# A hybrid attention and RG-LRU block: other portions for the RG-LRU's background steps, another call for placing attention's first tiles

## The chip, the core and the metric

The kernel runs on one core of one Trainium2 chip. The metric is the device time of one execution in microseconds. TensorE (PE) multiplies, VectorE (DVE), ScalarE (ACT) and GpSimd (POOL) do the elementwise work, and all DMAs are issued on one queue, that of SyncE (SP), in order.

## What is computed

One transformer block over 2048 tokens of width 1024 with a context of 256 tokens, all in float32. One input projection gives queries, keys and values of a differential attention (4 heads, two maps per head of 64 dimensions, values of 128) and, for the other half of the width, the input u and the gate g of an RG-LRU. Cut to its core:

```python
q, k, v, u, g = split_proj(h @ w_in)              # and the same of the context
q, k = apply_rope(q, cos, sin), apply_rope(k, cos, sin)
s = einsum(q, k_all) * ATT_SCALE                  # two maps m per head
p = softmax(s); a = p[0] - lam * p[1]
o = diff_head_norm(a @ v_all)
# RG-LRU, both directions d, 512 channels
u = centred_conv(u, conv_w, conv_b)
r, i = sigmoid(u @ w_gates[d] + b_gates[d])       # in blocks of 64 channels
log_a = -8 * r * softplus(-lru_lambda[d])
h_t = exp(log_a) * h_(t-1) + sqrt(-expm1(2 * log_a)) * i * u
y_lru = (h_forward + h_backward) * gelu(g)
y = concat(o, y_lru) @ w_out
x = layer_norm(alpha * x + g1 * y)                # then a SwiGLU, and a second norm
```

## The kernel before

**Stages.** Norms, modulation and the projection to u take the first 210 us; the other projections run to 700 us with the RG-LRU behind them; attention runs from 700 to about 1420 us; the output projection and the two FFN products fill the rest. Every float32 product is made of three matmuls on values split into a high and a low part (`mm3`, L141 to L144), so all activations and weights are split: `hi` and `lo` by ACT (L209) and POOL (L210) behind a projection, weights by ACT (L173) and DVE (L174).

**Projections.** The tokens are four blocks of 512, X = blocks 2 and 3 first, then Y = blocks 0 and 1, each with its activations `ht` in SBUF (two tiles, loaded in four DMAs each). One projection of 128 columns over one block is 24 matmuls into a PSUM tile `ps_p` (values: `ps_v`, four per block and pair of heads). A q or k projection is evacuated by ACT (a copy `kf`) and DVE (rope: the shuffle L203, products L204 and L205, sum L206), then split and stored; a value only needs ACT and one DVE step (L249). X runs g, v, k, q (32 calls of a background function, `between_x`), then Y runs g (8 calls), then head by head k, v and q in 24 calls of `between`.

**Background.** The RG-LRU is a generator, `chain()`, over four blocks of 128 channels: convolution, gate weights, gates (matmuls `ps_g`, ACT L571, POOL L573), the recurrence (DVE L603 to L624, with four long scans L620, L623, L621, L624), and the output (L629, L643 to L646). Each step yields a cost; `pump(n)` takes steps until costs of n have been taken, so n is the portion that a call deals out. The costs are 67.4 for a channel block, 269.6 for four; then the generator says "drained" and holds until the g projections of Y are done, and its tail (`lru_out_y`, the lines L665 and L669, 10.8 for all four blocks) takes their output to `oy_d`.

**Handover.** `over_lru` takes what is left of the chain, closes the LRU's memory, lays attention's first tiles (`k0`, `k1`, `q0`, four `e`, the ring `aR`, PSUM `psS`) into the same place, and issues the loads of the first query; in later calls `early` takes 24 steps of the first scores, two each. A step is four matmuls `ps_s` (L846), a DVE pass (L848), and at the third step an exponent on ACT (L853); six steps make a tile of 128 queries, which POOL then turns into the difference of the two maps (L861, three L864). The product with the values (`pt`, then `po`, L920 to L927) of the first tile begins after 32 steps.

**What sets the order.** The program is written in the order of the code, but a scheduler with a model of the engines' times then places the instructions of each engine, so a step written earlier may run later, and DMAs are placed on SP's one queue in the same way.

Of the kernel before, what the change touches and what calls it, by code (L numbers as in the profile page):

```python
# [60 lines left out]
def kernel(ctx: ExitStack, tc: tile.TileContext, x, cx, prm_d, wa1, wa2, b_ada, w_in, w_v, lqk,  # L61
# [91 lines left out]
    with ExitStack() as s12:  # L153
# [26 lines left out]
        def load_tabs(b):  # L180
            ct = rp.tile([P, 512], F32, tag="ct", name="ct")
            st = rp.tile([P, 512], F32, tag="st_", name="st_")
            dma(ct, cos_d[:, b * 512:(b + 1) * 512])
            dma(st, sin_d[:, b * 512:(b + 1) * 512])
            tabs[b] = ct, st
# [523 lines left out]
        def pump(n):  # L709

            state["due"] += n
            paces.append((last["act"], last["dve"]))
            act, dve = paces[max(0, len(paces) - 1 - 1)]
            while state["due"] > 0:
                if state["end"] or (state["hold"] and not state["g_done"]):
                    state["due"] = 0
                    return
                try:
                    with tc.issue_after(act), tc.issue_after(dve):
                        cost = next(bg)  # L720
                    if cost == "drained":
                        state["hold"] = True
                    else:
                        state["due"] -= cost or 1.0
                except StopIteration:
                    state["end"] = True
# [39 lines left out]

        def between_x():
            next(fold, None)
            pump(5.5)

        X, Y = [2, 3], [0, 1]

# [6 lines left out]
        for b in Y:  # L779
            load_ht(b)  # L780
            load_tabs(b)
        run_units([("g", c, Y) for c in range(4)], lambda: pump(5.5))
        state["g_done"] = True

        slots = {}
# [93 lines left out]
        calls = [0]  # L879

        def between():
            calls[0] += 1
            if calls[0] < 14:
                pump(5)
            elif calls[0] == 14:
                over_lru()
            else:
                for _ in range(2):
                    early()
# [3 lines left out]
        def early():  # L893
            if left[0]:
                left[0] -= 1
                next(first)
# [400 lines left out]
    with ExitStack() as s6:  # L1297
# [40 lines left out]
        for n in range(32):  # L1338
            hf, i = n // 16, n % 16
            c = slice(hf * 512, (hf + 1) * 512)  # L1340
# [99 lines left out]
```

## Time and profile before

| | |
|---|---|
| median of three runs | 2962.98 us (2962.23 to 2969.71) |
| the profiled execution | 2965.58 us, span 2963.8 us |
| PE busy | 2776.1 us, 94% |
| DVE busy | 1955.0 us, 66% |
| ACT busy | 1407.1 us, 47% |
| POOL busy | 1421.9 us, 48% |

The page says where the time goes by engine; the chain of work that ended last lies on PE for 67% of the span. As averages over stages these shares don't say which engine is waited for between 200 and 740 us, where the change lies; this is read from the windows, waits and timelines in the section of rows below. All times are microseconds from the span's start.

### The profile page before, as it was taken

The numbers are of one execution on the slowest core, as the hardware profiler recorded it, in microseconds if no ns is written. First come the engines' busy times: TensorE is split into PE (matmuls) and PEld (weight loads), VectorE is DVE, ScalarE is ACT, GpSimd is POOL, SyncE is SP. The second block draws the span as 40 slices with busy tenths as digits, with TensorE's granted clock in tenths as the row PEclk, the third lists the DMA queues.
The fourth block names the chain that finished last, engine by engine and source line by source line (L and its number), as shares of the span: only waits on it lengthen the run. The fifth ranks groups of instructions, "written<-read, shape, count | busy, mean of one in ns | idle before, by whom it ended". The sixth has DMA issues, their size and how long they took to land.

```text
span 2963.8 us, 37341 instructions
## 1 busy us (share of the span) xinstructions
PE 2776.1 (94%) x13452; PEld 2316.7 (78%) x13452; DVE 1955.0 (66%) x3202; ACT 1407.1 (47%) x1907; POOL 1421.9 (48%) x891
## 2 busy tenths in 40 slices
PE   8989889878999999999985999999999998999998
PEld 4868767766899999887864888887888886887886
DVE  7755796487899989986886655558655545225554
ACT  3537568744777777763344333334333324113332
POOL 2014643455788888861535444445444433222443
PEclk9999999989999999999997999999999999999999
DMA  8874636366132312135563222223222218434542
GB/s 332 313 217 167 215 116 256 113 219 184 36 85 64 81 58 70 54 140 195 193 200 114 93 86 82 84 84 104 93 82 82 84 52 291 146 129 162 172 165 93
DMA packets 223193, 407.94 MB, mean 138 GB/s; under 512 B 20888, under 2 KB 110104, under 8 KB 220448
## 3 DMA queue, kind: packets, MB, share of 16 engines
q1 hardware_dynamic: 223008, 405.55, 41.2%
q8 instruction: 106, 1.74, 0.2%
q14 instruction: 79, 0.65, 0.1%
HBM read 281.74 MB, written 123.75 MB: 137 GB/s over the span
## 4 chain that ended last, share of the span: by engine, by line
PE 67%; DVE 7%; ACT 3%; DMA 3%; issue 1%; POOL 1%; SPq 0%; ACTq 0%; DVEq 0%; POOLq 0%
PE ps L143 9%; PE ps L144 9%; PE ps L142 9%; PE ps_s L846 8%; PE ps_f L142 5%; PE ps_f L143 5%; PE ps_f L144 5%; PE pt L927 4%; PE po L921 2%; PE po L922 2%; PE po L920 2%; DMA w2r<-in_w 1%; DVE e L848 1%; PE ps_w L1050 1%; PE ps_l L1050 1%
## 5 line engine op out<-in xcount | busy, mean ns | idle before, releaser
L848 DVE TENSOR_SCALAR_CACHE_REDUCE e<-ps_s 128x768 f32<-128x768 f32 x384 | 359.6, 951 | 37.7 <-PE ps_s L846 29.6
L864 POOL TENSOR_TENSOR a<-e,e 128x768 f32<-128x768 f32 x192 | 349.2, 1848 | 17.2 <-PE pt L927 12.5
L846 PE MATMUL ps_s<-k,q 128*128 128x384 f32 x1536 | 336.7, 351 | 15.1 <-DVE e L848 13.7
L853 ACT ACTIVATE e<-e,nm 128x2304 f32<-128x2304 f32 x128 | 285.3, 2229 | 51.8 <-DVE nm L852 48.7
L846 PEld LDWEIGHTS ps_s<-k,q 128*128 128x128 f32 x1536 | 267.9, 191 | 31.0 <-DVE e L848 23.9
L1324 POOL TENSOR_TENSOR hid<-hf,hid 128x1408 fp32r<-128x1408 f32 x32 | 104.8, 3276 | 293.9 <-ACT hid L1323 293.9
L931 ACT CAST ah<-pt 128x512 fp32r<-128x512 f32 x288 | 165.8, 582 | 127.7 <-PE pt L927 125.4
L932 DVE TENSOR_TENSOR al<-pt,ah 128x512 fp32r<-128x512 f32 x288 | 195.7, 685 | 33.7 <-ACT ah L931 33.4
L1323 ACT CAST hid<-hf 128x1408 fp32r<-128x1408 f32 x64 | 87.8, 1375 | 248.0 <-PE ps_f L144 232.0
L861 POOL TENSOR_SCALAR e<-e,rr,rn 128x2304 f32<-128x2304 f32 x64 | 146.4, 2287 | 92.5 <-DVE nm L852 49.6
L142 PE MATMUL ps_p<-ht,w 128*128 128x512 f32 (+1 forms) x416 | 162.8, 392 | 16.0 <-DVE kf L204 10.8
L927 PEld LDWEIGHTS pt<-ident,a 128*128 128x128 f32 x1152 | 144.5, 141 | 42.0 <-POOL a L864 3.3
L927 PE MATMUL pt<-ident,a 128*128 128x128 f32 x1152 | 174.7, 274 | 2.6 <-POOL a L864 2.4
L1189 POOL TENSOR_TENSOR s<-w1r 128x512 f32<-128x512 f32 x44 | 58.0, 1317 | 233.5 <-DMA w1r<-in_w 228.2
L144 PE MATMUL ps_p<-ht,w 128*128 128x512 f32 (+1 forms) x416 | 161.8, 390 | 8.2 <-DVE w L174 8.2
L143 PE MATMUL ps_p<-ht,w 128*128 128x512 f32 (+1 forms) x416 | 161.5, 388 | 0.0
L210 POOL TENSOR_TENSOR lo<-kf,hi 128x512 fp32r<-128x512 f32 (+1 forms) x36 | 58.7, 1632 | 176.5 <-ACT hi L209 140.8
L1194 POOL TENSOR_TENSOR s<-w1r,s 128x512 f32<-128x512 f32 x44 | 73.1, 1661 | 126.9 <-DVE w__15147 L1199 5.6
L920 PE MATMUL po<-ah,v 128*128 128x512 f32 x288 | 126.3, 438 | 0.6 <-ACT ah L931 0.6
L921 PE MATMUL po<-al,v 128*128 128x512 f32 x288 | 116.9, 406 | 3.1 <-DVE al L932 1.4
L922 PE MATMUL po<-ah,v 128*128 128x512 f32 x288 | 114.5, 398 | 0.0
L1324 DVE TENSOR_TENSOR hid<-hf,hid 128x1408 fp32r<-128x1408 f32 x32 | 54.4, 1701 | 86.2 <-ACT hid L1323 86.2
(3085 smaller groups left out, 8258.8 us busy)
## 6 DMA issues: line engine op xcount, KB each, us to landing
w1r<-in_w SPq DMA_DIRECT2D x88, 512.0 KB, 3.5
hf<-hid_d SPq DMA_DIRECT2D x64, 704.0 KB, 4.2
hid_d<-hid SPq DMA_DIRECT2D x88, 256.0 KB, 2.2
wraw<-in_w_in SPq DMA_DIRECT2D x32, 512.0 KB, 5.1
adaw<-in_wa SPq DMA_DIRECT2D x32, 512.0 KB, 4.7
q<-q_d SPq DMA_DIRECT2D x64, 256.0 KB, 4.9
oy<-oy_d SPq DMA_DIRECT2D x16, 1024.0 KB, 6.2
x<-in_x SPq DMA_DIRECT2D x24, 512.0 KB, 8.9
```

The costliest lines, as they stand in the source:

```text
L142: PE.matmul(ps, lhsT=lh, rhs=rh, start=start, stop=False)
L143: PE.matmul(ps, lhsT=lh, rhs=rl, start=False, stop=False)
L144: last["pe"] = PE.matmul(ps, lhsT=ll, rhs=rh, start=False, stop=stop).ins
L846: PE.matmul(ps[:, j, :384], lhsT=q[:, m, part, qt * P:(qt + 1) * P], rhs=kst[h, m][:, c0:c0 + 384], start=(part == 0), stop=(part == 1))
L848: V.tensor_scalar(et[:, cc * 768:(cc + 1) * 768].rearrange("p (a b) -> p a b", a=2), ps[:, :, :384], -0.125, None, ALU.mult, ALU.min, accu ...
L853: S.activation(et, et, AF.Exp, bias=nm[:, m:m + 1], scale=-1.0, accum_out=ss[m])
L864: last["a"] = G.tensor_tensor(a, es[0][:, g * 768:(g + 1) * 768], es[1][:, g * 768:(g + 1) * 768], ALU.add).ins
L920: PE.matmul(po, lhsT=vh, rhs=ah, start=(j == 0), stop=False)
L921: PE.matmul(po, lhsT=vh, rhs=al, start=False, stop=False)
L922: PE.matmul(po, lhsT=vl, rhs=ah, start=False, stop=(j == NKT - 1))
L927: PE.transpose(pt[:, qt * P:(qt + 1) * P], ath[h, b, qt, j // 6][:, (j % 6) * P:(j % 6 + 1) * P], ident)
L932: V.tensor_tensor(al, pt, ah.bitcast(F32), ALU.subtract)
```

## The change

Three numbers and one condition change. A call in X and in Y's g projections deals out portions of 7 and not 5.5 (32 + 8 calls: 280 of cost and not 220, where the whole chain has 280.4), a call in the rest of Y 6 and not 5, and `over_lru` stands at the eleventh of those calls and not at the fourteenth, so that `early` begins with the twelfth.

```diff
--- before.py
+++ after.py
@@ -766,7 +766,7 @@
 
         def between_x():
             next(fold, None)
-            pump(5.5)
+            pump(7)
 
         X, Y = [2, 3], [0, 1]
 
@@ -779,7 +779,7 @@
         for b in Y:
             load_ht(b)
             load_tabs(b)
-        run_units([("g", c, Y) for c in range(4)], lambda: pump(5.5))
+        run_units([("g", c, Y) for c in range(4)], lambda: pump(7))
         state["g_done"] = True
 
         slots = {}
@@ -880,9 +880,9 @@
 
         def between():
             calls[0] += 1
-            if calls[0] < 14:
-                pump(5)
-            elif calls[0] == 14:
+            if calls[0] < 11:
+                pump(6)
+            elif calls[0] == 11:
                 over_lru()
             else:
                 for _ in range(2):
```

The two programs hold the same work; the scheduler places it otherwise. Up to some 380 us the order is nearly the same. The gates of channel block 2 stood between the first and third projection of Y and now stand between the fourth and eighth; those of block 3 move from the fourteenth to sixteenth to the seventeenth to twentieth (of 32). Three places follow, each before and after.

DVE at the end of X's keys, where the scans of channel block 1 (`L621` forward half, `L624` backward half) meet the rope of the keys (L203 to L206) and a weight split (`L174`), before:

```order
L621 SCALAR_TENSOR_TENSOR gate_3081<-A_3310,gate_3081 128x2048
L206 TENSOR_TENSOR kf<-kf,sh 128x512
L624 SCALAR_TENSOR_TENSOR gate_3083<-A_3311,gate_3083 128x2048
L174 TENSOR_TENSOR w<-wraw,w 128x1024
L204 TENSOR_TENSOR kf<-ps_p,ct 128x512
L205 TENSOR_TENSOR sh<-sh,st__1992 128x512
L203 STREAM_SHUFFLE sh<-kf 128x512
L206 TENSOR_TENSOR kf<-kf,sh 128x512
```

and after, from the same scan on:

```order
L621 SCALAR_TENSOR_TENSOR gate_2830<-A_3096,gate_2830 128x2048
L204 TENSOR_TENSOR kf<-ps_p,ct 128x512
L205 TENSOR_TENSOR sh<-sh,st__1992 128x512
L174 TENSOR_TENSOR w<-wraw,w 128x1024
L624 SCALAR_TENSOR_TENSOR gate_2832<-A_3097,gate_2832 128x2048
L203 STREAM_SHUFFLE sh<-kf 128x512
L206 TENSOR_TENSOR kf<-kf,sh 128x512
L204 TENSOR_TENSOR kf<-ps_p,ct 128x512
```

One `L204`, with its `L205`, moved from behind `L624` and `L174` to directly behind `L621`; the next `L204` stands behind all of them.

A little later, where X ends, SP's queue changes too: the loads `ht` of Y's first block stood one by one among stores of queries and of RG-LRU output, and now three of four stand in a row directly behind the store `hs_d` of block 1's recurrence; those of the second block stay together, and the gate weights' loads `gr` go from ahead of them to behind. On PE the first projection of Y was cut by 48 gate matmuls in three pieces; it now stands whole (24), then 6 matmuls of the second block, then 19 of the first block's next projection.

DVE at the end of the RG-LRU: `L665` and `L643` are its last products, L203 to L206 rope of q and k, `L249` the evacuation of a value, `L174` a weight split. Before:

```order
L665 TENSOR_TENSOR gg<-hs,gg 128x1024
L204 TENSOR_TENSOR kf<-ps_p,ct 128x512
L205 TENSOR_TENSOR sh<-sh,st__4121 128x512
L203 STREAM_SHUFFLE sh<-kf 128x512
L665 TENSOR_TENSOR gg<-gate_4402,gg 128x1024
L206 TENSOR_TENSOR kf<-kf,sh 128x512
L643 TENSOR_TENSOR gg<-gate_4402,gg 128x512
L204 TENSOR_TENSOR kf<-ps_p,ct 128x512
L205 TENSOR_TENSOR sh<-sh,st__4112 128x512
L174 TENSOR_TENSOR w<-wraw,w 128x1024
L643 TENSOR_TENSOR gg<-gate_4402,gg 128x512
L665 TENSOR_TENSOR gg<-hs,gg 128x1024
```

and after, from the longer scans on:

```order
L621 SCALAR_TENSOR_TENSOR gate_4129<-A_4385,gate_4129 128x2048
L206 TENSOR_TENSOR kf<-kf,sh 128x512
L624 SCALAR_TENSOR_TENSOR gate_4131<-A_4386,gate_4131 128x2048
L249 TENSOR_TENSOR vl<-ps_v,vh 128x512
L174 TENSOR_TENSOR w<-wraw,w 128x1024
L665 TENSOR_TENSOR gg<-hs,gg 128x1024
L665 TENSOR_TENSOR gg<-gate_4129,gg 128x1024
L643 TENSOR_TENSOR gg<-gate_4129,gg 128x512 x2
L174 TENSOR_TENSOR w<-wraw,w 128x1024
L249 TENSOR_TENSOR vl<-ps_v,vh 128x512 x2
L665 TENSOR_TENSOR gg<-hs,gg 128x1024
```

Before, the last products stood among the rope steps of q and k projections; now they stand among value evacuations, directly behind the two scans.

The handover, PE's end of the projections (`ps_p`) and its first scores (`ps_s`), to the first product with the values (`po`), before:

```order
L144 MATMUL ps_p<-ht,w 128x512
L846 MATMUL ps_s<-k,q 128x384 x16
L927 MATMUL pt<-ident,a 128x128 x2
L846 MATMUL ps_s<-k,q 128x384 x32
L927 MATMUL pt<-ident,a 128x128 x2
L846 MATMUL ps_s<-k,q 128x384 x12
L927 MATMUL pt<-ident,a 128x128 x2
L846 MATMUL ps_s<-k,q 128x384 x36
L927 MATMUL pt<-ident,a 128x128 x2
L920 MATMUL po<-ah,v 128x512
```

and after:

```order
L144 MATMUL ps_p<-ht,w 128x512
L846 MATMUL ps_s<-k,q 128x384 x56
L927 MATMUL pt<-ident,a 128x128 x2
L846 MATMUL ps_s<-k,q 128x384 x12
L927 MATMUL pt<-ident,a 128x128 x2
L846 MATMUL ps_s<-k,q 128x384 x36
L927 MATMUL pt<-ident,a 128x128 x2
L846 MATMUL ps_s<-k,q 128x384 x12
L927 MATMUL pt<-ident,a 128x128 x2
L846 MATMUL ps_s<-k,q 128x384 x8
L920 MATMUL po<-ah,v 128x512
```

Before this point the order had four groups of eight `ps_s` among the last four projections; there are none now, and all scores stand behind the projections. SP's queue at the same place, with the loads of the first query (`q_d_72`) and keys (`k_d_68`), before:

```order
L70 DMA k_d_70<-lo 128x512 x2
L70 DMA v_d_77<-vh 256x1x256
L70 DMA wraw<-in_w_in 128x1024
L70 DMA v_d_77<-vh 256x1x256
L70 DMA q<-q_d_72 64x2x512 x4
L70 DMA v_d_77<-vl 256x1x256
L70 DMA k<-k_d_68 64x2304 x4
L70 DMA v_d_77<-vl 256x1x256
L70 DMA v_d_77<-vh 256x1x256 x2
L70 DMA v_d_77<-vl 256x1x256
```

and after:

```order
L70 DMA q_d_74<-hi 128x512
L70 DMA oy_d_78<-gg 128x512
L70 DMA oy_d_79<-gg 128x512
L70 DMA v_d_77<-vl 256x1x256
L70 DMA q_d_74<-lo 128x512
L70 DMA q_d_74<-hi 128x512
L70 DMA k_d_71<-hi 128x512
L70 DMA q<-q_d_72 64x2x512 x4
L70 DMA k<-k_d_68 64x2304 x4
```

The loads stood ahead of most value stores of the second pair of heads and of every store of `k_d_71`; now they stand behind the value stores and the first store of `k_d_71`, the keys of the last head, of the fourth-last projection.

## Rows read from the trace of the kernel before

**Rows 1.** Windows; time, busy us (instructions) of PE, PEld, DVE, ACT, POOL, clock, DMA share.

```profile
600.00:700.00 100.00, 84.47 (x433) 73.18 (x432) 78.37 (x91) 40.16 (x52) 42.20 (x22) 0.91 0.64 209
...
700.00:740.00 40.00, 27.27 (x109) 19.48 (x107) 28.48 (x66) 21.04 (x21) 32.70 (x21) 0.91 0.65 189
...
800.00:900.00 100.00, 100.00 (x606) 91.46 (x605) 90.56 (x208) 75.22 (x96) 83.66 (x53) 1.00 0.34 90
```

**Rows 2.** Waits of PE from 300 to 700 us (total, times, longest); durations of line L174.

```profile
PE ps_p L142 <- DVE kf L204: 10.8, 2, 8.6
...
PE ps_v L142 <- ACT w L173: 10.0, 2, 6.0
...
PE ps_p L144 <- DVE w L174: 7.4, 6, 2.4
...
PE ps_g L142 <- ACT gate L571: 4.3, 2, 3.3
...
L174 DVE TENSOR_TENSOR w<-wraw,w x28: 1204/1226/2741, 251.4 to 675.6; 128x1024 fp32r<-128x1024 f32 x28
```

**Rows 3.** Timelines of DVE, POOL, PE near 430 us; start, duration, instruction, idle time before.

```profile
417.78 4.81 DVE L621 TENSOR_TENSOR_SCAN gate<-A,gate 128x2048 f32<-128x2048 f32 x1
...
423.10 4.47 DVE L624 TENSOR_TENSOR_SCAN gate<-A,gate 128x2048 f32<-128x2048 f32 x1
...
427.49 2.22 DVE L174 TENSOR_TENSOR w<-wraw,w 128x1024 fp32r<-128x1024 f32 x1
...
429.63 0.68 DVE L204 TENSOR_TENSOR kf<-ps_p,ct 128x512 f32<-128x512 f32 x1
...
428.59 7.33 POOL L629 TENSOR_TENSOR gate<-gate,gate 128x512 f32<-128x512 f32 x4
...
430.45 0.77 PE L142 MATMUL ps_p<-ht,w 128*128 128x512 f32 x1 [8.60 <-DVE kf L204]
```

**Rows 4.** Timeline of PE at 457 us; the tile `ht`, 425 to 480 us.

```profile
457.82 0.50 PE L142 MATMUL ps_p<-ht,w 128*128 128x512 f32 x1 [1.16 <-DMA ht<-ht_d]
...
DMA to landing us min/median/max: 7.9/10.1/13.1
```

**Rows 5.** A stretch as in rows 1; lines of DVE from 610 to 656 us.

```profile
615.00:655.00 40.00, 29.73 (x180) 27.62 (x179) 39.04 (x32) 12.58 (x17) 32.94 (x15) 0.87 0.64 230
...
L206 DVE TENSOR_TENSOR kf<-kf,sh 128x512 f32<-128x512 f32 x5 | 7.7, 1530 | 0.0
...
L643 DVE TENSOR_TENSOR gg<-gate,gg 128x512 f32<-128x512 f32 x2 | 4.6, 2302 | 0.0
```

**Rows 6.** Timelines of POOL, SP and PE at the handover, 649 to 701 us.

```profile
649.09 2.83 POOL L669 TENSOR_TENSOR gg<-gg,hs 128x1024 fp32r<-128x1024 f32 x1
...
659.58 2.72 SPq L70 DMA_DIRECT2D q<-q_d  x4
...
663.05 4.82 SPq L70 DMA_DIRECT2D k<-k_d  x4
...
676.37 1.66 PE L846 MATMUL ps_s<-k,q 128*128 128x384 f32 x8 [0.77 <-issue]
...
700.16 0.40 PE L143 MATMUL ps_p<-ht,w 128*128 128x512 f32 x1
...
700.39 0.40 PE L144 MATMUL ps_p<-ht,w 128*128 128x512 f32 x1
```

**Rows 7.** Attention's start: the tile `ps_s` on DVE, then timelines of DVE, POOL, PE.

```profile
L848 DVE TENSOR_SCALAR_CACHE_REDUCE e<-ps_s x32: 937/954/961, 681.6 to 743.1; 128x768 f32<-128x768 f32 x32
...
719.56 0.17 DVE L860 RECIPROCAL rr<-ss 128x1 f32<-128x1 f32 x1 [2.38 <-ACT e L853]
...
714.25 2.26 POOL L861 TENSOR_SCALAR e<-e,rr,rn 128x2304 f32<-128x2304 f32 x1 [2.15 <-DVE nm L852]
...
716.59 5.35 POOL L864 TENSOR_TENSOR a<-e,e 128x768 f32<-128x768 f32 x3
...
739.72 0.66 PE L920 MATMUL po<-ah,v 128*128 128x512 f32 x1 [0.56 <-ACT ah L931]
```

## The prediction, made before the changed kernel had run

> **What bounds the kernel now.** I read the busy time by stretch first [rows 1]. From 800 us on, inside attention, PE is busy 100.00 of 100 us at a granted clock of 1.00: nothing ahead of that can make it faster, only let it begin sooner. In the hundred before 700 it lacks 15.5 us and in the next forty 12.7, both at clock 0.91, and no other engine is full over such a stretch either. So the change is worth what the projections' end and the handover to attention move, and the instruction order from the first output of attention (its first `po` matmul, 739.72 [rows 7]) to the end of the program is the same but for a few neighbours. I therefore forecast the shift of that one instant and add it to the time.
>
> Second the waits of PE from 300 to 700 us [rows 2]: the long ones are on DVE, for the rope evacuation `kf` (L204, 10.8 us) and the weight split `w` (L174, 7.4), then on ACT, the split L173 (10.0) and the gates L571 (4.3). They are short waits of PE behind LRU work that stands ahead of the evacuations on the same engine. The clearest is at 430.45 [rows 3]: PE waits 8.60 us for an L204 that itself stood behind two scans (L621 4.81, L624 4.47) and an L174 of 2.22. The third view, the table of stretches around the LRU's last part [rows 5], has DVE busy 39.04 of the 40 us from 615 to 655 while PE does 29.73 at clock 0.87; before and behind it, DVE has room.
>
> **Portions in the last of X.** Up to about the seventh of the X keys (380 us) the order is nearly that of before, so I give nothing to the larger portions there. At channel block 1's end one L204 moves from behind L624 and L174 to directly behind L621. PE was free at 421.85 (430.45 less 8.60). L621 ends at 422.5, L204 takes 0.68, so PE goes on at about 423.2: a wait of 1.3 in place of 8.6. It then has one projection of 5.6 us (24 matmuls, 0.23 us from one start to the next in the last two of [rows 6]) and at 428.8 wants the next L204. That now stands behind an L205, L174, L624 and three short rope steps, about 0.6 + 2.2 + 4.4 + 0.6 + 0.6 + 0.6 = 9.0 us, thus ends at 432.2: a second wait of 3.4. Gain 8.6 - 1.3 - 3.4 = **-4** us. If the second wait is hidden, -7; if the contention that made L174 2.22 instead of 1.23 [rows 2] strikes the moved steps as well, +1.
>
> **From X to Y.** Before, PE had the gates of channel block 2 in pieces between the first Y projections while the activations came in. They now stand behind the fourth Y projection, and the `ht` loads stand in a row on SP. What they hid is the load: 7.9 to 13.1 us from issue to landing [rows 4], and PE waited only 1.16 us at 457.82. A first group of loads that stands earlier on SP comes earlier, if its buffers are free; the second group needs the last X projection finished, so its 10 us lie open except for the projections on the first block. These are 24 and 19 matmuls, some 10 us, where PE had 48 of gates (11 us) besides. I take **+2**, with 0 (the earlier issue pays for it) and +5 (a landing of 13.1 against 8 of cover) as bounds; the 1.16 is the nearest row. Behind the loads on SP wait the stores of the last X queries; these release `hi` and `lo`, and PE gets at them through L204 only, which is in that range.
>
> **The LRU's last part in Y.** Gates of block 2 move some four projections later, those of block 3 some four (from the 14th to 16th Y projections to the 17th to 20th), and the tail (L665, L643, L669) lands where value projections are evacuated and no longer between rope steps, as the DVE order shows. The cost of the LRU work does not change: two long scans of some 4.6 each [rows 3], the products L665, and 4.6 us of L643 [rows 5]. What changes is the company. Beside them DVE did the rope of five q/k blocks, of which L206 alone took 7.7 us [rows 5], the first of four lines; a block of values has one L249 in their place. PE lacked 10.3 of the 40 us from 615. With four value blocks in the place of four rope blocks DVE is relieved of L206's 1.5 us four times, 6 us, and of three other lines besides, and could give nearly all of that back: -10. Against it stand the weight splits, which keep their place between scans (L174 after L624 and again after L643) and were PE's other wait, and the gates' own waits on ACT, which come along with them. I take **-3**; bounds -10 and, if the later start only pushes the same jam against the last projections, +4.
>
> At this place a rule bears on the sum. The rows show L174 between 1.20 and 2.74 us (median 1.23) [rows 2], and one of the long ones, 2.22 at 427.49, beside POOL's L629 [rows 3]. The Trainium skill, page "SBUF — State Buffer", section "Who interferes with whom", says that a DVE instruction with two SBUF inputs contends with a GpSimd instruction that reads SBUF; the trace agrees in these rows. By that rule the tail's L669, L629 and L646 take their DVE partners' time with them wherever they are put, and this term would be 0.
>
> **Handover.** Before, the loads of the first query and keys go out at 659.58 and 663.05, behind the LRU's last L669 (649.09, 2.83 us); the first score matmul runs 13.3 us behind the issue of the first keys, at 676.37, between projections [rows 6]. Eight of the 32 score steps ahead of the first `po` were thus done by 700.8, and cost PE 8 x 0.83 = 6.6 us there (eight matmuls 1.66 [rows 6]). Without them the projections would have ended at 694.2, so `po` came 739.7 - 694.2 = 45.5 us behind. After, all projections end first; the loads stand on SP behind the store of a key block of the fourth-last projection. That is some 14 us before the end; four issues of query loads (2.72 us) and the same 13.3 put the first score step 2 us behind the end; I take 2.5 (bounds 0 and +6). From there I run the pipeline by rows: 0.8 for the first step's matmuls, six steps at about 1 us of DVE, the 2.38 for which L860 waits for the exponent and 0.6 of small steps around it, so the first L861 is at +10 [rows 7]. Then POOL takes 2.26 + 5.35 for L861 and three L864, 7.7 from 714.25 to 721.94, and 8.0 with the small step to the next tile, and `po` needs the fourth tile's first L864: 10 + 3 x 8.0 + 2.3 + 1.8 + 1.0 = 39.1. With 2.5 ahead that is 41.6; the end of the queue has one step less ahead of `po` (31 for 32), so one more comes after it, 0.8. Together 42.4 against 45.5: **-3**; I take -2, because the last projections' L210 splits still stand on POOL ahead of the second L861. Bounds -5 and +10.
>
> **Sum.** -4 + 2 - 3 - 2 = -7 us. The profiled execution took 2965.58 us (span 2963.8), 2.6 above the median of 2962.98; the shift is the same from either, 2965.58 - 7 = 2958.6 and by the median **2956.0**.
>
> **The rivals.** *Nothing that can be told* (the forecast's neighbour): the LRU's chain and its contention travel with the work, and what the first term gives the second and third take; 0 to -3, 2960 to 2963. The rule above leads here too: -4 + 2 + 0 - 2 = -4, 2959. For it speaks that the work is the same to the instruction; against it the 10.3 us of [rows 5].
>
> *More than forecast*: the tail among the values frees DVE (-8, the weight splits keep 2 of the 10), and the second wait of the first term is hidden (-7): -7 + 2 - 8 - 2 = -15, 2948. For it: DVE at 39.04 of 40 is the limit there, and rope work is what leaves. Against: L174 stays.
>
> *Slower*: the later tail holds the memory in which attention's first tiles are placed. Before, 8 us lay between the last L669 and the query loads, and projections covered nearly all of the 13.3 us that the keys took. After, tail and loads both stand some four projections (4 x 5.6 = 22 us) nearer to the projections' end. If a jam around the scans lets the tail end 10 us later than I place it, the keys' loads go out with the last projection: PE then has neither projections nor scores until they land. That costs 10 to 17 on top of the handover's -2, and the jam makes the third term +4: -4 + 2 + 4 + 8 = +10, up to +17; I take +11, 2974. It decides as soon as the first key load is issued less than about 9 us before the last projection's end.
>
> *The change does nothing*: excluded, the order changes at all three places.
>
> **How the numbers follow.** Forecast, -12 to -4: 0.45, most of it within 0.3% (8.9 us, about what a measurement of this kernel can tell from no change), a third of it beyond: 0.15 faster, 0.30 same. Nothing to tell: 0.13, same. More than forecast: 0.22, faster. Slower: 0.20, of it 0.18 beyond 0.3%, 0.02 same. Faster 0.37, same 0.45, slower 0.18. The range takes forecast and neighbour whole, the larger gain down to 2946 (about four fifths of it) and the slower case up to 2974 (under half): 0.45 + 0.13 + 0.17 + 0.07 = 0.82; the bounds of single terms lie inside.
>
> **What would show it.** First term: PE's wait at about 430 us split in two, with one L204 between the scans. Second: a wait of PE on `ht` of over 2 us. Third: PE busy more than 29.7 per 40 us around the last scans. Fourth: first score matmul 0 to 6 us behind the last projection, `po` 42 behind it. A key load issued after the last projection has begun its second half, or `po` later than 740, makes the forecast wrong.

## The result, and the profile after

The changed kernel takes 2984.68 us (2982.25 to 2987.27) where the kernel before, run beside it, takes 2962.61: a ratio of 1.007 [1.0051, 1.009], 0.7% or 22 us slower. Its profiled execution took 2987.27 us (span 2985.5), that of before 2965.58 (2963.8). The forecast of 2956.0, 7 us faster, has the wrong sign, and the time lies outside its range, 2946 to 2974.

The instant on which the forecast was built did move: the first `po` starts at 766.30 us and not at 739.72 [rows 7], 26.6 later. At the last `po` of attention 22.8 are left (1382.1 for 1359.3), and these go through to the end.

The windows of the changed kernel, columns as in [rows 1]:

```profile
600.00:700.00 100.00, 82.05 (x400) 69.59 (x400) 79.58 (x72) 66.11 (x80) 46.89 (x25) 0.86 0.51 176
700.00:740.00 40.00, 27.97 (x117) 21.43 (x115) 20.34 (x47) 14.51 (x16) 15.15 (x12) 0.92 0.95 268
800.00:900.00 100.00, 99.79 (x595) 90.21 (x594) 91.71 (x216) 76.01 (x94) 91.21 (x58) 1.00 0.26 65
```

Attention from 800 us on is full, as before. Between 600 and 700 PE does 400 instructions for 433, at a lower clock. The waits of PE from 300 to 700 us of the changed kernel (in total, times, longest) answer [rows 2]:

```profile
PE ps_v L142 <- ACT w L173: 16.5, 5, 5.6
PE ps_p L142 <- DVE vl L249: 8.3, 3, 6.0
PE ps_p L142 <- DMA ht<-ht_d: 7.2, 1, 7.2
PE ps_p L144 <- DVE w L174: 7.2, 7, 1.8
...
PE ps_p L142 <- DVE kf L204: 2.6, 2, 1.5
```

The wait of 10.8 on the rope L204 is down to 2.6, which is what the change was read to do. Three others have come: one load `ht`, a value evacuation L249, and 6.5 more on the weight split of ACT. PE's timeline of the changed kernel shows the first place and the second (answering [rows 3] and [rows 4]):

```profile
413.96 0.50 PE L142 MATMUL ps_p<-ht,w 128*128 128x512 f32 x1 [1.46 <-DVE kf L204]
...
422.45 0.60 PE L142 MATMUL ps_p<-ht,w 128*128 128x512 f32 x1 [2.74 <-ACT A L606]
...
430.84 0.47 PE L142 MATMUL ps_p<-ht,w 128*128 128x512 f32 x1 [1.09 <-DVE kf L204]
...
458.69 0.39 PE L144 MATMUL ps_p<-ht,w 128*128 128x512 f32 x1
466.32 0.77 PE L142 MATMUL ps_p<-ht,w 128*128 128x512 f32 x1 [7.24 <-DMA ht<-ht_d]
466.89 0.63 PE L143 MATMUL ps_p<-ht,w 128*128 128x512 f32 x1
```

SP's queue ahead of that load, changed kernel:

```profile
453.53 1.47 SPq L70 DMA_DIRECT2D oy_d<-gg  x2
456.69 0.33 SPq L70 DMA_DIRECT2D wraw<-in_w_in  x1
...
459.15 2.82 SPq L70 DMA_DIRECT2D ht<-ht_d  x4
...
468.80 2.94 SPq L70 DMA_DIRECT2D gr<-in_w_g  x2
```

The last projection of X, whose buffer the load takes, ends at 451.0. The load goes out 8.1 us later (before: 4.4), behind two RG-LRU stores, a weight and two rope tables (`ct`, `st`), and its first part lands 7.0 after that, at 466.19. Of these 15 us one projection covers 7.

The stores aren't what makes the load late. In this program a DMA on SP takes up the semaphore (the counter that tells that a DMA has landed) of the eighth DMA before it, as 1025 of the 1049 do in either kernel, and waits until that one has landed. The store at 453.53 went out when the third load of the first block had landed (453.47), the weight at 456.69 when the fourth had (456.63). SP's waits from 447 to 457 us of the changed kernel show it:

```profile
SPq L70 <- DMA ht<-ht_d: 5.5, 3, 2.5
```

And before the change the same load came no sooner. SP's queue and PE there, kernel before:

```profile
454.13 6.63 SPq L70 DMA_DIRECT2D ht<-ht_d  x4
...
465.89 0.33 SPq L70 DMA_DIRECT2D st__4121<-in_sin  x1
```

```profile
469.22 0.39 PE L142 MATMUL ps_p<-ht,w 128*128 128x512 f32 x1
```

The table at 465.89 waits for the load at 454.13, which landed at 465.83: 16.1 us behind X's last projection, where the changed kernel has 15.2. But PE had one projection and 48 gate matmuls to do meanwhile and began the next projection at 469.22 without a wait. What the change took away is the work in front of the load, not the load's time.

The end of the RG-LRU on DVE and the two waits of PE there, changed kernel (answering [rows 5]; the window's columns as in [rows 1]):

```profile
650.00:690.00 40.00, 31.36 (x159) 27.35 (x160) 38.75 (x25) 15.41 (x19) 26.84 (x11) 0.79 0.70 244
```

```profile
668.90 2.29 DVE L665 TENSOR_TENSOR gg<-hs,gg 128x1024 f32<-128x1024 f32 x1
672.37 2.30 DVE L665 TENSOR_TENSOR gg<-gate,gg 128x1024 f32<-128x1024 f32 x1 [1.18 <-POOL gate L629]
674.59 4.55 DVE L643 TENSOR_TENSOR gg<-gate,gg 128x512 f32<-128x512 f32 x2
679.07 3.36 DVE L174 TENSOR_TENSOR w<-wraw,w 128x1024 fp32r<-128x1024 f32 x1
682.35 1.28 DVE L249 TENSOR_TENSOR vl<-ps_v,vh 128x512 fp32r<-128x512 f32 x2
```

```profile
667.55 0.47 PE L142 MATMUL ps_p<-ht,w 128*128 128x512 f32 x1 [1.90 <-DVE vl L249]
...
683.17 0.77 PE L142 MATMUL ps_p<-ht,w 128*128 128x512 f32 x1 [5.97 <-DVE vl L249]
```

DVE is as full as it was (38.75 of 40), now around 670 and not 635, and a value's evacuation (two L249 of 0.64 each) stands behind 13.4 us of the RG-LRU's products and a weight split.

The handover in the changed kernel, from the timelines of SP, PE, ACT and POOL (answering [rows 6] and [rows 7]):

```profile
701.62 2.60 SPq L70 DMA_DIRECT2D q<-q_d  x4
704.62 2.39 SPq L70 DMA_DIRECT2D k<-k_d  x4
...
716.18 3.98 PE L846 MATMUL ps_s<-k,q 128*128 128x384 f32 x12 [2.84 <-DMA k<-k_d]
...
724.63 1.28 ACT L853 ACT_TABLE_LOAD   x1
...
730.79 2.27 POOL L861 TENSOR_SCALAR e<-e,rr,rn 128x2304 f32<-128x2304 f32 x1 [2.19 <-issue]
...
739.80 2.27 POOL L861 TENSOR_SCALAR e<-e,rr,rn 128x2304 f32<-128x2304 f32 x1
...
751.67 2.27 POOL L861 TENSOR_SCALAR e<-e,rr,rn 128x2304 f32<-128x2304 f32 x1 [3.89 <-DVE rr L860]
...
766.30 0.40 PE L920 MATMUL po<-ah,v 128*128 128x512 f32 x1
```

To add such places up I use one table. A **loss** is the time between two ends of projections less what the matmuls begun between them take at full clock (0.227 us from start to start for 512 columns), so it holds waits and low clock together. Projections are numbered through; 31 to 37 end X, 38 to 45 are Y's g, 46 to 51 the first keys and values, 52 to 59 rope work (q, k, q, k), 60 to 65 the second values and the queries behind them, 66 to 69 the last head. All in us, worked out from the matmuls of each profiled execution:

| kernel | 12-30 | 31-37 | 38-45 | 46-51 | 52-59 | 60-65 | 66-69 | to 800 | to last `po` | last `po` at |
|---|---|---|---|---|---|---|---|---|---|---|
| before | 19.4 | 16.3 | 3.2 | 7.9 | 15.2 | 15.8 | 2.0 | 33.3 | 80.5 | 1359.3 |
| after | 25.4 | 11.7 | 13.2 | 11.2 | 7.5 | 29.0 | -0.1 | 35.3 | 83.3 | 1382.1 |
| x7_only | 22.7 | 13.9 | 13.7 | 11.2 | 6.8 | 27.9 | 0.1 | 36.0 | 82.9 | 1380.8 |
| w2_late | 18.4 | 15.7 | 10.6 | 0.3 | 8.3 | 25.3 | 0.0 | 36.9 | 79.3 | 1362.0 |
| after_no_ht1 | 21.0 | 13.4 | 2.4 | 8.1 | 6.7 | 24.2 | 0.5 | 43.8 | 78.5 | 1364.8 |
| after_no_tail | 21.8 | 13.4 | 12.8 | 11.2 | 6.0 | 13.3 | 7.3 | 30.0 | 80.7 | 1362.6 |
| before_no_tail | 19.5 | 16.6 | 4.1 | 8.0 | 16.0 | 10.5 | 0.3 | 23.9 | 77.3 | 1343.7 |
| after_v_late | 21.5 | 11.7 | 13.3 | 11.2 | 7.5 | 17.6 | 15.4 | 34.0 | 81.8 | 1379.9 |
| after_neither | 22.5 | 13.9 | 1.9 | 9.0 | 4.5 | 17.9 | 1.2 | 36.4 | 78.8 | 1354.0 |

The 22.8 us at the last `po` are thus +6.0 - 4.6 + 10.0 + 3.3 - 7.7 + 13.2 - 2.1 + 2.0 + 2.8. The first column is unsure: over the kernels that keep before's X it runs from 18.4 to 24.1, over those with the changed X from 19.0 to 25.4. Of its +6.0, 2.8 stand at projection 12, which ends at 259.3 for 256.6. Every engine's order is the same in both kernels up to 277 us, and so are PE's waits there; only the clock differs, as the windows of before and of the changed kernel show. These 2.8 belong to the execution, not to the change:

```profile
245.00:260.00 15.00, 12.42 (x53) 9.58 (x53) 8.74 (x10) 9.64 (x15) 8.70 (x8) 1.00 0.48 149
245.00:260.00 15.00, 12.35 (x41) 9.33 (x40) 8.67 (x10) 7.59 (x11) 6.97 (x5) 0.77 0.42 123
```

### The profile page after: what moved, and what is told of

Its sections match the earlier page's. It is cut to its first block, busy times and chain, and to the rows that moved or that the text cites. A ratio compares the mean times of both kernels' runs of the same rounds, so it can differ in the third digit from the quotient of the medians.

```text
span 2985.5 us, 37341 instructions
## 1 busy us (share of the span) xinstructions
PE 2785.9 (93%) x13452; PEld 2321.3 (78%) x13452; DVE 1952.5 (65%) x3202; ACT 1402.5 (47%) x1903; POOL 1421.8 (48%) x891
## 4 chain that ended last, share of the span: by engine, by line
PE 67%; DVE 7%; ACT 5%; DMA 4%; issue 3%; POOL 2%; SPq 0%; DVEq 0%; ACTq 0%; POOLq 0%
PE ps L143 9%; PE ps L142 9%; PE ps L144 9%; PE ps_s L846 8%; PE ps_f L142 5%; PE ps_f L143 5%; PE ps_f L144 5%; PE pt L927 4%; PE po L921 2%; PE po L922 2%; PE po L920 2%; DMA w2r<-in_w 2%; PE ps_w L1050 1%; PE ps_l L1050 1%; PE ps_l L1051 1%
## 5 line engine op out<-in xcount | busy, mean ns | idle before, releaser
L846 PE MATMUL ps_s<-k,q 128*128 128x384 f32 x1536 | 338.5, 352 | 17.6 <-DVE e L848 13.2
L861 POOL TENSOR_SCALAR e<-e,rr,rn 128x2304 f32<-128x2304 f32 x64 | 146.4, 2287 | 88.2 <-DVE nm L852 52.9
L142 PE MATMUL ps_p<-ht,w 128*128 128x512 f32 (+1 forms) x416 | 164.8, 397 | 22.8 <-DVE vl L249 8.3
L144 PE MATMUL ps_p<-ht,w 128*128 128x512 f32 (+1 forms) x416 | 164.4, 396 | 8.1 <-DVE w L174 8.1
L143 PE MATMUL ps_p<-ht,w 128*128 128x512 f32 (+1 forms) x416 | 163.7, 393 | 0.0
L920 PE MATMUL po<-ah,v 128*128 128x512 f32 x288 | 125.7, 436 | 0.0
L142 PEld LDWEIGHTS ps_p<-ht,w 128*128 128x128 f32 x416 | 81.5, 196 | 43.4 <-issue 12.2
```

The costliest lines, as they stand in the source:

```text
L142: PE.matmul(ps, lhsT=lh, rhs=rh, start=start, stop=False)
L143: PE.matmul(ps, lhsT=lh, rhs=rl, start=False, stop=False)
L144: last["pe"] = PE.matmul(ps, lhsT=ll, rhs=rh, start=False, stop=stop).ins
L846: PE.matmul(ps[:, j, :384], lhsT=q[:, m, part, qt * P:(qt + 1) * P], rhs=kst[h, m][:, c0:c0 + 384], start=(part == 0), stop=(part == 1))
L920: PE.matmul(po, lhsT=vh, rhs=ah, start=(j == 0), stop=False)
```

## The experiments

The expectations call theories by letters. A: the gate weights' load `gr`, which came late on SP, is the cause. B: the eleventh call. C: the larger portions. D: larger portions in X lose nothing, and a late RG-LRU is not dear. E: the hole at Y's entry together with the late tail; E1 says that the tail is dear because it stands beside values, E2 that it costs the same wherever it stands. G: a single delay is paid once, so that undoing its causes one by one gives back more than both together. What isn't in this list is told in the expectation itself.

**Which of the edits.** X's portion alone, the rest of the change alone, and a smaller step of the first:

```diff
 # x7_only, from before; x575_only has 5.75
         def between_x():
             next(fold, None)
-            pump(5.5)
+            pump(7)
```

> Only the portion of the 32 calls in X becomes 7; the calls in Y keep 5.5 and 5, the first tiles are placed at the fourteenth call. Theory A (the load of channel block 2's gate weights falls behind Y's activation loads on SP's queue, the whole RG-LRU runs 30 to 40 us later, its tail meets the last projections): the X portion alone does that, so the time is the changed kernel's, 2978 to 2990 us, with the block 2 gates starting near 488 us. Theory B (placing attention's tiles at the eleventh call is what costs): as before, 2955 to 2970. Theory C (larger portions everywhere put LRU steps ahead of evacuations): between, about 2970 to 2980.

```diff
 # call11_only, from before
-            if calls[0] < 14:
-                pump(5)
-            elif calls[0] == 14:
+            if calls[0] < 11:
+                pump(6)
+            elif calls[0] == 11:
                 over_lru()
```

> X and Y's g projections keep 5.5; only the portion of 6 in the rest of Y and the placing at the eleventh call are taken over. Theory A: gate weights of block 2 stay ahead of Y's second activation loads, so as before, 2955 to 2970 us. Theory B: the changed kernel's time, 2978 to 2990. Theory C: 2963 to 2972.

> The kernel before with X's portion at 5.75 in place of 5.5 and nothing else. The order of gates, loads and first scores is then that of the changed kernel. Theory E: the time jumps with the order and not with the size of the portion, 2976 to 2988 us. Rival (portions cost in proportion): about 2966 to 2969, a sixth of the way.

x7_only: 2983.75, 1.006 [1.0045, 1.0075]; its PE order is that of the changed kernel. call11_only: 2967.05, 1.0006 [0.9996, 1.0015]. x575_only: 2986.61, 1.0075 [1.0058, 1.0092]. X's portion does it all; by the time, the eleventh call and Y's portions move nothing, neither alone nor on top of it. By the time 5.75 is as dear as 7, too. That is in part chance: x575_only's last `po` is at 1374.4, 15.1 us behind before where x7_only has 21.5, and the rest of its time is a wait in the output projection (told with after_neither below). A sixth of 21.5 would be 3.6, so the loss doesn't go by the size of the portion: the scheduler's order flips between 5.5 and 5.75, and most of the loss comes with that.

**The load of the gate weights.** `gr` shares a buffer with the RG-LRU's output tiles, and went out at 468.80 in place of 443.81: its buffer was cleared at 461.67, behind the stores at 453.53, and then SP waited for the eighth DMA before it, a part of the load `ht`, to land (468.73). Once it got a buffer of its own, once the load `ht` was held behind it:

```diff
 # after_gr_own, from after
-            gr = lp.tile([P, 4, P], F32, tag="ul", name="gr", bufs=2)
+            gr = lp.tile([P, 4, P], F32, tag="gr", name="gr")
```

> The changed kernel, but the gate weights have a buffer of their own and no longer wait for one that the RG-LRU's output uses, so that their load stands on SP ahead of all of Y's activation loads. Theory A: block 2's gates start at 455 us or earlier, the tail ends before 655, the first scores run among the last projections again, and the time is 2945 to 2968 us. Theory B: the tiles are still placed at the eleventh call, 2978 to 2990. Theory C: portions stay 7 and 6, 2975 to 2988.

```diff
 # after_gr_first, from after; last["gr", 2] is the load of block 2's gr
-            load_ht(b)
+            if b == 1:
+                with tc.issue_after(last["gr", 2]):
+                    load_ht(b)
+            else:
+                load_ht(b)
```

> The changed kernel with all its portions and the eleventh call, but the loads of Y's second block are held until block 2's gate weights have been loaded, so that on SP the gate weights stand ahead of them as before; no buffer is added. Theory A (the place of that one load on SP sets the changed kernel's time): the gates of blocks 2 and 3 and the first scores stand where they stood in the kernel before, first po at 735 to 750 us, time 2955 to 2970. Theory D (a late RG-LRU is not dear in itself, as the kernel with the held gate weights showed; what costs are the larger portions in X): 2975 to 2988.

after_gr_own: 2982.54, 1.0057 [1.004, 1.0074], with 12.1 us lost at Y's entry, where PE waits 7.3 us for weight splits and gates and no longer for the load. By its time A misses. But the order came as A had it: block 2's gates start at 442.00, the last L669 at 644.02, the first scores at 671.63, among the last projections. And attention begins and ends far earlier than in the changed kernel, as the line L920 shows, first in the changed kernel, then in after_gr_own (the last two times are its first and last start):

```profile
L920 PE MATMUL po<-ah,v x288: 387/420/774, 766.3 to 1381.6; 128*128 128x512 f32 x144
L920 PE MATMUL po<-ah,v x288: 387/474/776, 744.5 to 1364.2; 128*128 128x512 f32 x144
```

That is 17.4 us at the last start, 5 behind before. Up to 7 of them may be the executions: the profiled one of after_gr_own was 4.4 us below its median, that of the changed kernel 2.6 above. Behind attention after_gr_own loses some 7 us against before, with a wait from 1480 to 1540 us that the changed kernel doesn't have:

```profile
PE ps_w L1050 <- DVE x L1070: 7.5, 1, 7.5
```

after_gr_first: 2982.67, 1.0051 [1.0036, 1.0066], its last `po` at 1381.9. `gr` goes out at 461.15 there, still 17 us later than before, and the wait only changed its name, as PE's timeline of after_gr_first shows:

```profile
468.92 0.79 PE L142 MATMUL ps_g<-uh,gh 128*128 128x512 f32 x1 [11.27 <-ACT gh L552]
```

So the order of the two loads on the queue isn't the cause: whichever goes first, PE waits for the other. A in its wider sense, the late gate weights, isn't refuted. With them early, half or more of the loss at the end of attention is gone; that this shows in the time, no run has shown.

**Is a late RG-LRU dear in itself?** The background is held ahead of block 2's gates until Y's loads are written, in before and in after:

```diff
 # w2_late (from before) and w2_late_after (from after)
+                    if c == 1:
+                        yield "w2"
...
-                if state["end"] or (state["hold"] and not state["g_done"]):
+                if state["end"] or (state["hold"] and not state["g_done"]) or (state["w2"] and not state["ht_y"]):
...
+        state["ht_y"] = True
```

> The kernel before with all its portions (5.5, 5.5, 5, fourteenth call); the background only stops ahead of block 2's gate weights until Y's activation loads are written. Theory A: the order gets the late RG-LRU without any larger portion, block 2's gates start at 470 us or later, first score behind the last projection, 2973 to 2988 us. Theories B and C: nothing of theirs is in it, 2958 to 2968.

> The changed kernel's portions (7, 7, 6, eleventh call) with the background held ahead of block 2's gate weights until Y's loads are written. The order of gates and loads is the changed kernel's. Theory A: nothing is gained over the changed kernel, 2978 to 2988 us, because the hold takes away none of the lateness. Theory D (portions in X): the hold undoes what the larger portions do in the last of X, 2962 to 2972.

w2_late: 2965.41, 1.0 [0.9991, 1.0009]. w2_late_after: 2980.13, 1.0045 [1.0031, 1.0059]. In w2_late the second half of the RG-LRU runs 9 to 30 us later than in before (first gates at 462.34 for 453.78, last L621 at 637.79 for 608.86), and the losses are those of the changed kernel at Y's entry (10.6) and at the end (25.3). Yet the time is that of before, because the stretch 46 to 51 loses 0.3 where before lost 7.9 and after 11.2. So lateness as such isn't dear; after has its two losses and doesn't get this return. There ACT is the engine: in the changed kernel block 2's activations and a weight split stand in one row, from ACT's timeline:

```profile
532.12 1.28 ACT L641 ACT_TABLE_LOAD   x1
533.42 0.63 ACT L641 ACTIVATE gg<-gg 128x512 f32<-128x512 f32 x1
533.96 1.24 ACT L601 ACTIVATE gate<-gate,spm 128x1152 f32<-128x1152 f32 x1
...
535.57 1.04 ACT L173 CAST w<-wraw 128x1024 fp32r<-128x1024 f32 x1
```

PE waited 5.57 us for that L173, until 536.66.

**The hole at Y's entry, priced.** Block 1 of Y reads block 3's activations, which are in SBUF, so its load and the wait for it are gone:

```diff
 # after_no_ht1 (from after), before_no_ht1 (from before)
-            load_ht(b)
+            if b == 1:
+                hts[b] = hts[3]
+            else:
+                load_ht(b)
```

> The changed kernel without the four loads of Y's second block: its projections take the activations of X's last block instead (that part of the result is left wrong). Theory E (PE stands idle at Y's entry because the first block's projections are done, the second block's activations are on their way and block 2's gates are not yet there to fill in; then the delayed RG-LRU meets the last values and the handover): the hole of 7 to 11 us goes, the rest stays, 2968 to 2978 us. Theory F (the whole loss comes from the late tail and the handover, the hole is paid back later): 2980 to 2986.

> The kernel before without the same loads. Theory E: there the gates fill the wait, so 0 to 4 us are gained, 2960 to 2966 us. Theory F: the same small change in both kernels.

after_no_ht1: 2969.03, 1.0015 [1.0005, 1.0026]. Against 1.007 this is 16 us less, and 17.3 at the last `po`. Of these the entry has 10.8: its loss falls from 13.2 to 2.4. Another 4.4 stand at 12 to 30, ahead of the load, and can't be its doing. From 440 to 512 us the waits of PE are only these:

```profile
PE ps_p L144 <- DVE w L174: 1.5, 1, 1.5
PE ps_p L142 <- ACT w L173: 0.5, 1, 0.5
```

before_no_ht1: 2979.25, 1.0048 [1.0032, 1.0064]. At the entry it loses 3.5, as before does with the load (3.2): there the load had cost nothing. That it is slower lies elsewhere, at 46 to 51 (20.1 for 7.9, waits on L173 of 5.6 and 8.3) and in the output projection (below), where the scheduler came to another order. The control is good for the entry alone.

**The tail, priced.** The tail's arithmetic (the gelu, L665, L668, L669) is left out:

```diff
 # after_no_tail (from after), before_no_tail (from before)
-            S.activation(gg, gg, AF.Gelu_apprx_tanh)
-            V.tensor_tensor(gg, hs, gg, ALU.mult)
-            S.copy(yh, gg)
-            G.tensor_tensor(yl, gg, hs, ALU.subtract)
```

> The changed kernel without the arithmetic of the RG-LRU's tail (the GELU, the products L665, the split L668 and L669 for blocks 0 and 1 are left out; their loads and stores stay). It prices what the tail costs where it stands. Theory A: PE's waits of 3.4 and 6.8 us for value evacuations at the 64th and 65th projections (some 15 us with the lowered clock) go, the key loads go out earlier, 2958 to 2972 us. Theory D: the tail is not the cause, 2976 to 2986.

> The kernel before without the same arithmetic, for comparison. Theory A: its tail stands among rope steps and costs PE a part of the 10.3 us it waits there: 2950 to 2960 us, a smaller gain than the changed kernel gets. Theory D: the same gain as in the changed kernel.

after_no_tail: 2961.88, 0.9993 [0.9982, 1.0003]. before_no_tail: 2946.4, 0.9931 [0.9916, 0.9946]. The wait of 5.97 is gone with the tail; what PE waits for between 655 and 695 us in after_no_tail is this:

```profile
660.37 0.47 PE L142 MATMUL ps_p<-ht,w 128*128 128x512 f32 x1 [0.27 <-DVE vl L249]
...
662.14 0.50 PE L144 MATMUL ps_p<-ht,w 128*128 128x512 f32 x1 [1.06 <-DVE w L174]
...
687.82 2.93 PE L842 MATMUL ps_s<-k,q 128*128 128x384 f32 x8 [4.08 <-DMA k<-k_d]
```

But the tail costs 0.8% where it now stands and 0.7% where it stood, about 23 and 20 us; in before it is paid in smaller pieces, 5.3 at 60 to 65 and 9.4 on the way into attention. Its new place makes a difference of a few us at most: without their tails the two kernels still lie 18.9 apart at the last `po` (1362.6 for 1343.7), so most of the 22.8 isn't the tail's.

**Is it the values?** The values of the second pair of heads go behind the queries:

```diff
 # after_v_late (from after), before_v_late (from before), w2_late_v_late (from w2_late)
-... for k in ("kvq" if c % 2 == 0 else "kq")], between)
+... for k in {0: "kvq", 2: "kqv"}.get(c, "kq")], between)
```

> The changed kernel with the second pair of heads' values projected behind head 2's queries and no longer ahead of them, so that the RG-LRU's tail stands beside q projections and the value evacuations (L249) come clear of it. Theory E1 (it is the value evacuations behind the tail on DVE that cost 15 us at the 64th and 65th projections): 2968 to 2978 us. Theory E2 (the tail costs its DVE time beside any evacuation; the place of the values does not matter): 2979 to 2990.

> The kernel before with the same exchange. Its tail stands ahead of the values; the exchange puts two more q projections beside it. Theory E1: slower by 0 to 8 us, 2963 to 2973. Theory E2: within 4 us of before.

> The kernel before with the background held ahead of block 2's gate weights (which cost nothing) and the values behind head 2's queries. Theory E1: of the 15 us at the 64th and 65th projections 5 to 12 come back, 2953 to 2961 us, faster than both kernels. Theory E2: 2962 to 2970.

after_v_late: 2983.18, 1.0055 [1.0039, 1.0071]. before_v_late: 2963.59, 0.999 [0.998, 0.9999]. w2_late_v_late: 2977.51, 1.0038 [1.0025, 1.005]. With values out of its way the tail's loss goes from 60-65 (29.0 to 17.6) to 66-69 (-0.1 to 15.4), now at a weight split; the largest wait of after_v_late:

```profile
686.15 0.79 PE L142 MATMUL ps_p<-ht,w 128*128 128x512 f32 x1 [9.49 <-ACT w L173]
```

E1 falls and E2 stands. The time of w2_late_v_late is longer than either foresaw, by a wait told below; its last `po`, 1361.6 for w2_late's 1362.0, hasn't moved, as E2 has it. Nothing of this makes a kernel that is faster than before by more than a measurement tells.

**One delay or two.** Both leave-outs together, and Y's first two g units by block, so that block 0's work comes first:

```diff
 # after_neither: the edits of after_no_ht1 and after_no_tail in one
 # before_gsplit, from before
-        run_units([("g", c, Y) for c in range(4)], lambda: pump(5.5))
+        run_units([("g", c, [b]) for b in Y for c in (0, 1)], lambda: pump(5.5))
+        run_units([("g", c, Y) for c in (2, 3)], lambda: pump(5.5))
```

> The changed kernel without the second block's loads (X's last block stands in) and without the tail's arithmetic, as in the two single runs. Theory E (the hole at Y's entry and the tail are two separate losses): the gains of 15.6 and 22 us add up, 2943 to 2953 us, what the kernel before reaches without its tail (2946). Rival G (they are one delay that is paid once): about 2960.

> The kernel before with Y's first two gate projections done for the first block and then for the second, so that more work on the first block stands ahead of the second block's loads. Theory E: in the kernel before the gates already fill that wait, so no change beyond 5 us, 2958 to 2970.

after_neither: 2964.26, 0.9995 [0.9985, 1.0004]. By the time alone it gives back no more than after_no_tail. But its last `po` is at 1354.0: 28.1 us ahead of after's, where the load alone gave 17.3 and the tail alone 19.5. The rest is lost later, in the output projection from 1480 to 1540 us, where the changed kernel's PE is busy 60.00 of 60 us and after_neither has this wait:

```profile
PE ps_w L1049 <- DVE x L1069: 7.5, 1, 7.5
```

The same wait of 7.5 stands in after_gr_own, x575_only, before_no_ht1 and w2_late_v_late, whose times are about that much too long for what they test: behind the last `po` these five take 1608 to 1614 us, the other kernels 1597 to 1606. At the end of attention 28.1 lies midway between the 19.5 that G asks and the sum of 36.8 that two separate losses would give. So neither G nor E holds alone: about half of the smaller gain is the same delay. before_gsplit: 2973.15, 1.003 [1.0018, 1.0042]; its entry loses 5.4, so that order is no cure.

## Why the prediction was wrong

**The sum.** The four terms came to -4.6 + 10.0 + 3.4 + 2.0 = +10.8 where the forecast had -7. The other 12.1 of the 22.9 (+6.0 at 12 to 30, +3.3 at 46 to 51, +2.8 behind 800 us) stood in no term; 2.8 of the first are the execution's.

**Reading.** That the change is worth what the first `po` moves held nearly: 26.6 at the first, 22.8 at the last, 21.7 in the span. About 7 of what the handover loses ahead of the first `po` come back by 800 us; the shift should have been taken at 800.

**Portions in the last of X: the place right, the size partly luck.** Forecast -4, measured -4.6 (x7_only -2.4, same order). One L204 stands between the scans, as described, and the wait of 8.60 is down to 1.09. The second wait, of 3.4, didn't come; one of 2.74 on ACT's L606, which I hadn't priced, made up for it. What went unread is that the scans move as well: L624 runs at 432.78 and not 423.10 [rows 3], and with it every store and every later step of the RG-LRU.

**From X to Y: the term that was mis-sized.** Forecast +2, at most +5; measured +10.0. The step said that the second block's load lies open "except for the projections on the first block", 24 and 19 matmuls, some 10 us of cover. Two things failed. The load was priced at some 10 us from X's end, its time from issue to landing; from X's end to its first landing it took 15.2, because SP's queue doesn't issue it when its buffer is free but behind what stands ahead of it, and that waits for the loads of the first block to land. It took as long before (16.1), so the late RG-LRU isn't the reason. And of the cover only the 24 counted, as a matmul of the second block stands ahead of the 19. The row leaned on, 1.16 us [rows 4], was no near row: it was a wait on the first block's load, as the second block's went out from 454.13 and landed from 465.83, and for that one PE hadn't waited at all. after_no_ht1 shows the size: of the 16 us by which it is shorter, the entry's own part is 10.8.

**The RG-LRU's last part in Y: sign wrong, size inside its bounds.** Forecast -3 (-10 to +4). From 52 to 69 the sum is 7.5 + 29.0 - 0.1 against 15.2 + 15.8 + 2.0, so +3.4. The relief of DVE was there where the chain had stood (-7.7, the -8 of the rival with the larger gain), and was more than taken back where it now stands (+13.2). The bound of +4 was set for the case that "the later start only pushes the same jam against the last projections", and that is what happened. A rule was weighed there, and by it this term would be 0, as the cost goes wherever the work is put: the Trainium skill, page "SBUF — State Buffer", section "Who interferes with whom", says that a DVE instruction with two SBUF inputs contends with a GpSimd instruction that reads SBUF. The trace agrees in kind: L665 took 2.3 us three times beside POOL's L629 or L646, and 1.22 at 651.66 with POOL idle; L174 took 3.36 beside L669 and L646, and 1.20 at 418.64 with POOL idle. Not priced at all were the +3.3 at 46 to 51: the gates' activations, moved there, stand ahead of a weight split on ACT. I had named those waits, and put no number to them.

**Handover: the loads right, partly by luck, the pipeline not.** Forecast: first score 2.5 us behind the last projection; measured 2.84. Two errors cancel in it: the keys went out 8.7 us ahead of the end and not some 11.3, and the score ran 11.6 behind their issue and not 13.3. So the rival *Slower* had its condition met (its point was 9), but not its price: the wait it set at 10 to 17 was 2.84. From the first score to the first L861 I took 10 and it took 14.6, because the last projections' rope (L204 at 720.00, L206 at 723.21) stands between the score passes on DVE and a table load of 1.28 ahead of the first exponent; the tiles then came 9.0, 11.9 and 8.1 apart, not 8.0. With 1.5 more at the end, `po` was 53 and not 42.4 behind the last projection. Run from rows of a pipeline in its steady state, its start came out 10 us short. By 800 us only +2.0 of it is left, against the -2 of the forecast.

**Clock: left out of every term.** I summed waits, but PE's clock falls behind the long ones (last section).

**Not settled.** Why the scheduler's order flips between 5.5 and 5.75; how much of the other 3.2 at 12 to 30 is the change; how far the late gate weights alone make the loss, as after_gr_own's time is spoiled further on; and how the lost return at 46 to 51 would be had with larger portions, since w2_late_after didn't get it (14.4 there).

## What to carry to other kernels

Work that fills PE is also cover for the loads around it: when a change moves it away, take from the trace how long the load needs from the freeing of its buffer to its landing, with all that stands ahead of it on the in-order queue, and take off the work that is left in front. The wait that the cover left over doesn't show this. When a step moves, follow its stores and the loads that share its buffers one stage further. And where a scheduler sets the order, try two sizes of the number that is changed: if the smallest step does most of it, the order is what was changed, not the portion. Such kernels are better compared at the end of the stage under test than by their whole time: here five of them met a wait of 7.5 us some 140 us behind it, which the others don't have.

## What the hardware showed

Two of the waits of PE cost more than their length. Behind the 7.24 us at the entry and the 5.97 us at 683, PE's clock is granted at about half, the lower of its two levels (1.2 GHz for 2.4), as these windows of the changed kernel show (the clock is the third number from the right):

```profile
451.00:459.00 8.00, 5.97 (x25) 4.35 (x24) 6.36 (x9) 2.68 (x4) 1.37 (x2) 1.00 1.03 403
466.00:471.00 5.00, 4.68 (x12) 3.76 (x13) 0.58 (x1) 0.00 (x0) 0.00 (x0) 0.56 1.03 413
471.00:476.00 5.00, 5.00 (x23) 4.14 (x23) 0.00 (x0) 0.62 (x1) 0.00 (x0) 1.00 1.02 392
```

```profile
683.00:688.00 5.00, 4.83 (x11) 3.80 (x12) 4.96 (x7) 1.64 (x2) 2.76 (x3) 0.50 0.60 225
```

Matmuls of 0.39 us take 0.63 there (466.89 above), and 12 and 11 begin in such five microseconds where 23 do at full clock: some 2 us on top of each of the two waits, a third more. Behind the short waits of 0.52 and 1.51 us in the first of these windows the clock stays at 1.00.

The windows also show the loads at their limit: in these three, between 451 and 476 us, the 16 DMA engines are full (share 1.02 to 1.03) at 392 to 413 GB/s. In the kernel before they are as full over these 25 us, 1.04 at 403 GB/s. The eight loads `ht` issued from 440.78 to 461.0 have 1 MB each, 8.4 MB or 21 us at that rate.
